# Norm statistics by accumulation, a reworked spatial gating and a richer scheduler model in a two-layer trunk kernel

## The chip, the cores and the metric

The kernel runs on the eight cores of one Trainium2 chip. The metric is the device time of one execution in microseconds (us), taken from the slowest core. Most executions agree within 0.3%. Some executions fall into a second, slower state, in which the cores of one die, sometimes of both, have a lower granted TensorE clock, that is, a lower share of the full clock at which the tensor engine may run (for example 0.93 to 0.95 against 0.98 to 0.99 in the run after that took 1251.35 us; in the run of `e12_best` that took 1307.13 us, 0.95 to 0.97 on one die and 0.89 to 0.90 on the other). A median that is given here is over all runs of its kernel, slow ones included, unless the text says otherwise.

Before the change the median was 1233.7 us (four runs, 1233.03 to 1415.23, the last one slow).

## The reference, cut to what matters

One inference step of two layers. Layer 0 mixes tokens with windowed attention beside a short gated convolution. Layer 1 mixes them with a chunked gMLP ("spatial gating"). Each is followed by a gated ConvFFN, and each sub-layer begins with an RMS norm with adaLN modulation.

```python
def rms_norm(x, g):
    y = x * lax.rsqrt(jnp.mean(x * x, axis=-1, keepdims=True) + EPS)
    return y * g

def modulate(x, g, shift, scale):
    return rms_norm(x, g) * (1 + scale) + shift

def gmlp_mixer(h, w_in, v_g, w_s, b_s, w_out):
    u, v = jnp.split(jax.nn.gelu(h @ w_in), 2, axis=-1)
    v = rms_norm(v, v_g).reshape(B, nc, CHUNK, GMLP_GROUPS, GMLP_GROUP_DIM)
    s = jnp.einsum('gts,bnsgc->bntgc', w_s, v) + b_s.T[:, :, None]
    return (u * s.reshape(B, T, GMLP_WIDTH)) @ w_out

def conv_ffn(h, w_up, conv_w, w_down):
    g, val = jnp.split(dwconv3(h @ w_up, conv_w), 2, axis=-1)
    return (jax.nn.silu(g) * val) @ w_down

# per layer: x = x + gate * mixer(modulate(x)); x = x + gate2 * conv_ffn(modulate(x))
```

The width is 1024, the FFN's inner width 2816. Each core holds 512 context tokens (tiles named P: `xP`, `hP`, `uP`) and some 1150 latent tokens with the halo that windows and convolutions need (tiles named S: `xS`, `hS`, `uS`).

## The kernel before

Activations lie feature-major: 1024 features are 8 chunks of 128 partitions, tokens run along the free axis. The sum over features of an RMS norm is therefore a sum over partitions. Before the change, it is done on the tensor engine: eight matmuls with a matrix of ones (value 1/1024) add the eight chunks of squares in PSUM, and the result is already broadcast over all partitions.

```python
class Norm:
    def sq(self, k, eng="act"):              # square of chunk k into the h tile
        P.act(h_(self.st, k), self.xf(k), AF.Square)
    def stat(self, k):                       # eight of these per norm
        if k == 0:
            self.b = BK.take(); BK.reserve(self.b)
        P.mm(bk(self.b, 0, self.st.n), ones, h_(self.st, k), start=(k == 0), stop=(k == KC - 1))
    def fin(self):                           # rsqrt as exp(-0.5 * ln(x))
        n = self.st.n
        r = self.rs[:, 0:n]
        P.act(r, bk(self.b, 0, n), AF.Ln, bias=eps)
        P.act(r, r, AF.Exp, scale=-0.5)
        BK.give(self.b)
    # apply(k): multiply by rs, then scale and shift, into h (the next matmul's operand)

def residual(nm, l, m, st, b, k, stat=True):   # after each output-projection block
    P.stt("dve", x_(st, k), bk(b, 0, st.n), mod_(l, m, k, st.j), x_(st, k), ALU.mult, ALU.add)
    if nm is not None:
        nm.sq(k)
        if stat:
            later(lambda: nm.stat(k), 2)
```

A norm's `fin` and its eight `apply` steps go into a queue, `side`, from which the main loop takes a few after every block of matmuls.

Spatial gating of layer 1, for 13 chunks of up to 128 tokens (v is token-major here, so its norm is along the free axis):

```python
def v_item(ch):                              # 16 matmuls, two Gelu, one sum of squares
    ...
    for i in range(2):
        P.act(ch["gv"][:, i * 512:(i + 1) * 512], bk(b2[i], 0, 512), AF.Gelu_apprx_tanh)
    P.add("dve", ... scalar_tensor_tensor(junk, gv, 1.0 / D, gv, mult, mult, accum_out=ssq[:, c:c+1]))
def v_stats(chs):                            # for a batch of 3 or 4 chunks
    P.act(rsv[:, a:z], ssq[:, a:z], AF.Ln, bias=eps)
    P.act(rsv[:, a:z], rsv[:, a:z], AF.Exp, scale=-0.5)
def v_norm(ch):
    P.stt("dve", ch["vn"].whole(), ch["gv"].whole(), rsv[:, c:c + 1], gvn.whole(), ALU.mult, ALU.mult)
def sp_item(ch):                             # 8 spatial matmuls, bias, gate product
    ...
        P.tt("dve", tv, <psum>, bsp..., ALU.add)
        P.tt("pool", uv, uv, tv, ALU.mult)
```

Finally, the program does not emit instructions in the order in which it is written. It records operations with their dependencies, and a list scheduler simulates the five engines with a cost model and takes, on each engine, the ready operation of the highest priority. The resulting order of each engine is fixed in the program. The model's numbers therefore matter only through the order which they produce:

```python
LAT = {"pe": 130.0, "act": 160.0, "dve": 130.0, "pool": 130.0, "sp": 100.0}   # ns, by producer
...
            else:
                busy = op.cost
                end = t + busy
...
                elif o.eng == op.eng and not o.is_dma:
                    r = end if e == "pe" or i not in o.raw else end + 90.0
                else:
                    r = end + LAT[e]
```

In the trace before, ScalarE loads an activation table at its first operation and wherever its work changes between `Ln`/`Exp` and the FFN's `Silu` or the gating's `Gelu`: 15 loads of 1.28 us. The model before knows nothing of that.

Of the kernel before, what the change touches and what calls it, by code (L numbers as in the profile page):

```python
# [9 lines left out]
F32 = mybir.dt.float32  # L10
BF16 = mybir.dt.bfloat16
AF = mybir.ActivationFunctionType
ALU = mybir.AluOpType
ESZ = {F32: 4, BF16: 2}
ENGINES = ("pe", "act", "dve", "pool", "sp")
LAT = {"pe": 130.0, "act": 160.0, "dve": 130.0, "pool": 130.0, "sp": 100.0}
DMA_RATE = 300.0


# [75 lines left out]
class Op:  # L95
    __slots__ = ("idx", "eng", "emit", "deps", "raw", "is_dma", "sig", "sem", "semval", "waits", "pre", "key",
                 "cost", "prio", "start", "pos", "end")

    def __init__(self, idx, eng, emit, is_dma):
        self.cost = 0.0  # L100
        self.prio = idx
        self.start = 0.0
        self.idx = idx
        self.eng = eng
        self.emit = emit
        self.deps = set()
        self.raw = set()
        self.is_dma = is_dma
        self.sig = False
        self.sem = None  # L110
        self.semval = None
        self.waits = ()
        self.pre = None
        self.key = None


class Prog:
# [112 lines left out]
    def schedule(self):  # L230
# [11 lines left out]
        free = {e: 0.0 for e in ENGINES}  # L242
        dma_free = 0.0
        for op in ops:
            if left[op.idx] == 0:
                heapq.heappush(wait[op.eng], (0.0, op.prio, op.idx))
# [3 lines left out]
        while ev:  # L250
# [16 lines left out]
            if op.is_dma:  # L267
                busy = 600.0 if e == "pool" else 60.0
                dma_free = max(dma_free, t + busy + 1300.0) + op.cost / DMA_RATE
                end = dma_free + 600.0  # L270
            else:
                busy = op.cost
                end = t + busy
            op.end = end
            free[e] = t + busy
            heapq.heappush(ev, (free[e], e))
            for j in succ[i]:
                o = ops[j]
                if op.is_dma:
                    r = end  # L280
                elif o.eng == op.eng and not o.is_dma:
                    r = end if e == "pe" or i not in o.raw else end + 90.0
                else:
                    r = end + LAT[e]
                ready[j] = max(ready[j], r)
# [13 lines left out]
    def act(self, out, in_, func, bias=None, scale=None, accum_out=None):  # L299
# [9 lines left out]
        if accum_out is not None:  # L309
            writes.append(accum_out)  # L310
            kw["accum_out"] = accum_out.ap
        return self.add("act", lambda e: e.activation(out.ap, in_.ap, func, **kw), reads=reads, writes=writes)  # L312

# [169 lines left out]
def build():  # L483
# [40 lines left out]
    with es:  # L524
# [214 lines left out]
        class Norm:  # L739
            def __init__(self, l, which, st, tmps, rs, x=None):  # L740
                self.l, self.w, self.st = l, which, st
                self.tmps, self.rs = tmps, rs
                self.xf = x if x is not None else (lambda k: x_(st, k))
                self.b = None

            def sq(self, k, eng="act"):
# [6 lines left out]
            def stat(self, k):  # L753
# [3 lines left out]
                P.mm(bk(self.b, 0, self.st.n), ones, h_(self.st, k), start=(k == 0), stop=(k == KC - 1))  # L757

            def fin(self):
                n = self.st.n  # L760
                r = self.rs[:, 0:n]
                P.act(r, bk(self.b, 0, n), AF.Ln, bias=eps)
                P.act(r, r, AF.Exp, scale=-0.5)
                BK.give(self.b)
# [25 lines left out]

        def residual(nm, l, m, st, b, k, stat=True):
            P.stt("dve", x_(st, k), bk(b, 0, st.n), mod_(l, m, k, st.j), x_(st, k), ALU.mult, ALU.add)
            if nm is not None:
                nm.sq(k)
                if stat:
                    later(lambda: nm.stat(k), 2)
# [285 lines left out]

        def oproj_item(l, key, src, st, nm, k, last, m=2, stat=True):
            w = use((key, k))
            b = BK.take()
            for kk in range(KC):
                P.mm(bk(b, 0, st.n), w[:, kk, :], src(st, kk), start=(kk == 0), stop=(kk == KC - 1))
            residual(nm, l, m, st, b, k, stat)
            if last:
                release((key, k))  # L1090
# [40 lines left out]
        def act_pair(out, b, ap, func, scale):  # L1131
            r = both(b, ap)
            return P.add("act", lambda e: e.activation(out.ap, ap, func, scale=scale), reads=r, writes=[out])  # L1133

# [50 lines left out]
        while al:  # L1185
            m, q = al.popleft()
            fill.append(lambda m=m, q=q: ada_item(0, m, q))
        nA = [Norm(0, 1, SP, None, None), Norm(0, 1, S0, None, None)]

        def oproj_a(st, nm, k):  # L1190
            assert all(bl.get("done") for bl in blocks[:8])
            oproj_item(0, "we", mx_, st, nm, k, False, stat=False)

# [40 lines left out]
        for i, nm in enumerate(nA):  # L1234
            nm.tmps, nm.rs = tA, rA[i]
            for k in range(KC):
                nm.stat(k)
            queue_apply(nm)
        ATAIL = O_W + NFC * 1664 * 2 - 12288
        tB = [P.tile(f"tB{i}", [128, NP], F32, ATAIL + 2048 * i) for i in range(4)]  # L1240
        rB = [P.tile(f"rB{i}", [128, NP], F32, ATAIL + 8192 + 2048 * i) for i in range(2)]
        nB = [Norm(0, 1, S1, tB, rB[0]), Norm(0, 1, S2, tB, rB[1])]
        for k in range(KC):
# [85 lines left out]
        F0 = ([SP, St(0, 0, 384)], [St(0, 384, 768), St(0, 768, 1152)])  # L1329
        flush()  # L1330
        for nm in nB:
            queue_apply(nm, PO8, AC8)

        def norms_l1(g, ft):
            if g == 0:
                tms = [ft[0][0], ft[0][1], ft[1][0], ft[1][1]]
                rss = [ft[2][0], ft[2][1]]
            else:
                tms, rss = l1t["tm"], l1t["rs"]
            return [Norm(1, 0, st, tms, rss[i]) for i, st in enumerate(F0[g])]  # L1340

# [36 lines left out]
        P.dma("sp", bsp.whole(), dr(d_bsp.ap()))  # L1378
        P.dma("pool", wst.whole(), dr(d_wst.ap()))
        for nm in keepB:  # L1380
            queue_apply(nm)

# [3 lines left out]
        def u_item(k, st, last):  # L1386
            w = use(("u", k))
            b = BK.take()
            for kk in range(KC):
                P.mm(bk(b, 0, st.n), w[:, kk, :], h_(st, kk), start=(kk == 0), stop=(kk == KC - 1))  # L1390
            P.act(u_(st, k), bk(b, 0, st.n), AF.Gelu_apprx_tanh)
            if last:
# [6 lines left out]
        def v_item(ch):  # L1399
            st, cbk = ch["st"], ch["c"]  # L1400
            ch["gv"] = gv[gi[0] % 6]
            ch["i"] = gi[0]
            gi[0] += 1
# [6 lines left out]
            for i in range(2):  # L1410
                P.act(ch["gv"][:, i * 512:(i + 1) * 512], bk(b2[i], 0, 512), AF.Gelu_apprx_tanh)
            c = ch["i"]
            P.add("dve", lambda e, a=ch["gv"], c=c: e.scalar_tensor_tensor(  # L1413
                junk.h[:, :], a.h[:, :], 1.0 / D, a.h[:, :], ALU.mult, ALU.mult, accum_out=ssq.h[:, c:c + 1]),
                reads=[ch["gv"].whole()], writes=[junk.whole(), ssq[:, c:c + 1]])

        def v_stats(chs):
            a, z = chs[0]["i"], chs[-1]["i"] + 1
            P.act(rsv[:, a:z], ssq[:, a:z], AF.Ln, bias=eps)
            P.act(rsv[:, a:z], rsv[:, a:z], AF.Exp, scale=-0.5)  # L1420

# [8 lines left out]
        def sp_item(ch):  # L1430
# [3 lines left out]
            for gh in range(2):  # L1434
# [9 lines left out]
                uv = ut[:, gh * 4:gh * 4 + 4, t0:t0 + nt_]  # L1444
                P.tt("pool", uv, uv, tv, ALU.mult)

        junk = P.tile("junk", [128, D], BF16, n1 + 10240)
        assert n1 + 10240 + 2048 <= O_END, n1 + 12288 - O_END

# [3 lines left out]
        side_all()  # L1453
        chP = [dict(st=SP, c=i) for i in range(4)]
        chS = [dict(st=G0, c=i) for i in range(9)]
        spq = deque()

        def v_batch(chs):
            for ch in chs:
                emit(lambda: v_item(ch))  # L1460
                if spq:
                    c2 = spq.popleft()
                    v_norm(c2)
                    emit(lambda: sp_item(c2))
            later(lambda: v_stats(chs))
            spq.extend(chs)

        v_batch(chP)
        v_batch(chS[0:3])
        for k in range(KC):  # L1470
            for st in (G1, G2):
                emit(lambda: u_item(k, st, st is G2))
            if spq and k % 2 == 1:
                c2 = spq.popleft()
                v_norm(c2)
                emit(lambda: sp_item(c2))
        v_batch(chS[3:6])
        v_batch(chS[6:9])
        release(("v", 0))
        release(("v", 1))  # L1480
        flush()
        H0, H1, H2 = St(0, 0, 383), St(0, 383, 704), St(0, 704, 1024)
        nA = [Norm(1, 1, st, l1t["tiles"][0:3], l1t["tiles"][3 + i]) for i, st in enumerate((SP, G0))]
        for k in range(KC):
            for st, nm in ((SP, nA[0]), (G0, nA[1])):
                emit(lambda: oproj_item(1, "wo", u_, st, nm, k, False))
                if spq and k < 4:
                    c2 = spq.popleft()
                    v_norm(c2)
                    emit(lambda: sp_item(c2))  # L1490
        flush()
        for nm in nA:
            queue_apply(nm)
        nB = [Norm(1, 1, st, None, None) for st in (G1, G2)]
        for k in range(KC):
# [167 lines left out]
```

## Time and profile before

| what | before |
|---|---|
| time, median of fast runs | 1233 us |
| tensor engine (PE) busy | 1142.7 us of 1232.2 (93%), 7225 matmuls |
| VectorE (DVE), ScalarE (ACT), GpSimd (POOL) busy | 763.3, 607.5, 423.9 us |
| norm statistics | 17 norms with 8 ones-matmuls each, 136 matmuls |

From the page of the profiled run (slowest core): the span, the busy time of each engine with its share and number of instructions, and by engine the chain of work that ended last.

```profile
span 1232.2 us, 21546 instructions; the slowest of 8 cores (1225.8 to 1232.2 us)
PE 1142.7 (93%) x7225; PEld 630.5 (51%) x7225; DVE 763.3 (62%) x1281; ACT 607.5 (49%) x1072; POOL 423.9 (34%) x489
...
PE 79%; DVE 8%; issue 5%; DMA 4%; ACT 4%; POOL 1%; DVEq 0%; ACTq 0%; POOLq 0%; SPq 0%
```

The kernel is bound by PE, and 79% of the last chain is matmul. There are two ways to gain: fewer matmuls, or less of the 89.5 us in which PE stands idle. The busy table by stretches of time tells where these are. Its first columns are the stretch and its length, then the busy time of each engine with the number of instructions, then the granted clock.

```profile
core 3: us, PE busy (x) PEld busy (x) DVE busy (x) ACT busy (x) POOL busy (x), PEclk, DMA share, GB/s
0.00:75.00 75.00, 26.80 (x226) 13.59 (x226) 26.62 (x58) 24.75 (x42) 17.08 (x30) 0.94 0.92 181
75.00:313.00 238.00, 214.32 (x1305) 99.03 (x1305) 148.79 (x251) 153.76 (x242) 72.66 (x84) 0.94 0.38 68
...
757.00:845.00 88.00, 79.86 (x496) 43.30 (x495) 57.60 (x71) 36.30 (x64) 38.95 (x37) 1.00 0.31 52
```

In the first 75 us weights and inputs arrive (DMA share 0.92), and PE idles 48 us. In projections and attention it idles 24 us, in spatial gating 8.1 us (88.00 less 79.86), between 375 and 660 us, in the first FFN, nothing.

The waits of PE in spatial gating (730 to 850 us), by what it waited for: total, number, longest.

```profile
PE ps L296 <- DVE vn L336: 5.2, 5, 1.7
PE ps L296 <- ACT uP L312: 1.8, 1, 1.8
PE ps L296 <- DVE tg L315: 1.6, 3, 0.7
...
```

So the wait that costs most is that for the normalised v (`vn`). Two things precede `vn`. One is the rsqrt on ScalarE with a table load before and behind it, as ScalarE's timeline shows (start, duration, instruction):

```profile
772.40 0.60 ACT L312 ACTIVATE gv<-ps 128x512 f32<-128x512 f32 x1 [1.13 <-PE ps L296]
773.00 1.28 ACT L312 ACT_TABLE_LOAD   x1
774.30 0.30 ACT L312 ACTIVATE rsv<-ssq,cf 128x4 f32<-128x4 f32 x1
774.68 0.20 ACT L312 ACTIVATE rsv<-rsv 128x4 f32<-128x4 f32 x1
774.91 1.28 ACT L312 ACT_TABLE_LOAD   x1
```

At the first of these loads one activation ends at 773.00 us and the next starts at 774.30, so this switch cost 1.30 us.

The other is the product on VectorE itself. The groups of instructions by shape (count, then busy us, then mean ns of one, then idle time before them):

```profile
L336 DVE SCALAR_TENSOR_TENSOR vn<-gv,rsv,gvn 128x1024 bf16<-128x1024 f32 x13 | 21.2, 1652 | 6.4 <-ACT rsv L312 6.4
L1413 DVE SCALAR_TENSOR_TENSOR junk<-gv 128x1024 bf16<-128x1024 f32 x13 | 18.8, 1443 | 29.0 <-ACT gv L312 29.0
L315 POOL TENSOR_TENSOR uS<-uS,tg 128x512 bf16<-128x512 bf16 x16 | 20.6, 1315 | 19.5 <-DVE tg L315 19.4
L312 ACT ACT_TABLE_LOAD x15 | 19.2, 1283 | 16.2 <-PE ps L296 6.3 <-DVE junk L1413 5.7 <-DMA cf<-cf 4.1
```

The mean of `vn` is 1652 ns, but single ones range from 1.27 us to 2.15 us, the long ones where a gate product of GpSimd (`uS<-uS,tg`) runs beside them.

### The profile page before, as it was taken

To read this page: it belongs to the slowest core of one execution; us is meant where nothing else is said; L and a number is where in the kernel's file an instruction comes from. 1 tells how busy PE (TensorE), PEld (TensorE's weight loads), DVE (VectorE), ACT (ScalarE), POOL (GpSimd) and SP (SyncE) were. 2 spreads that over 40 slices of the span, in tenths; PEclk is the share of its full clock that TensorE was granted. 3 is DMA by queue.
4 is the path that set the end of the run, shared out by engine and by line. 5 is a ranking of instruction groups with operands and counts; after the bars stand their busy time and mean duration, and the time that the engine had idled before them with its cause. 6 is when DMAs were issued, how large, how long until landed. Compare 5 with 4: busy or idle time off the path is not lost.

```text
span 1232.2 us, 21546 instructions; the slowest of 8 cores (1225.8 to 1232.2 us)
## 1 busy us (share of the span) xinstructions
PE 1142.7 (93%) x7225; PEld 630.5 (51%) x7225; DVE 763.3 (62%) x1281; ACT 607.5 (49%) x1072; POOL 423.9 (34%) x489
## 2 busy tenths in 40 slices
PE   1478899898999999999999999998999999999999
PEld 1235533333545555555555554544556555555566
DVE  3179765444679888888511522756788898893111
ACT  2257566667696555555312435443875555551000
POOL 2136512210374444444200321543554444442000
PEclk9889999989899999999999999999999999999999
DMA  9882254640313577776354560143306332225661
GB/s 182 173 199 44 35 86 67 103 71 1 52 18 57 96 123 138 124 134 119 65 103 86 92 131 7 21 68 59 52 1 103 55 65 50 48 48 110 141 136 56
DMA packets 32604, 102.27 MB, mean 83 GB/s; under 512 B 3312, under 2 KB 10096, under 8 KB 32112
## 3 DMA queue, kind: packets, MB, share of 16 engines
q0 software_dynamic: 23616, 85.21, 40.9%
q1 hardware_dynamic: 8880, 15.69, 3.9%
q8 instruction: 60, 0.98, 0.3%
q14 instruction: 48, 0.39, 0.1%
HBM read 179.27 MB, written 6.82 MB: 151 GB/s over the span
## 4 chain that ended last, share of the span: by engine, by line
PE 79%; DVE 8%; issue 5%; DMA 4%; ACT 4%; POOL 1%; DVEq 0%; ACTq 0%; POOLq 0%; SPq 0%
PE ps L296 79%; DMA w_ada<-ada 3%; DMA xS<-xs 1%; DVE cvt L336 1%; DVE nd L315 1%; DVE vn L336 1%; ACT pt L1133 1%; ACT L312 1%; ACT hS L312 1%; DVE pt L315 1%; DVE xS L336 0%; DVE nn L342 0%; DVE junk L1413 0%; DVE c L342 0%; DVE tm L315 0%
## 5 line engine op out<-in xcount | busy, mean ns | idle before, releaser
L336 DVE SCALAR_TENSOR_TENSOR ft<-ps,cf,ft 128x510 f32<-128x510 f32 (+5 forms) x704 | 424.3, 631 | 70.1 <-ACT ft L312 29.2
L296 PE MATMUL ps<-hS,w_up 128*128 128x386 bf16 (+4 forms) x2112 | 334.6, 318 | 0.1
L296 PEld LDWEIGHTS ps<-hS,w_up 128*128 128x128 bf16 x2112 | 206.2, 98 | 126.9 <-issue 0.6
L312 ACT ACTIVATE ft<-ps,cf 128x384 f32<-128x384 f32 (+4 forms) x354 | 200.3, 586 | 76.6 <-PE ps L296 76.0
L296 PE MATMUL ps<-hP,w_up 128*128 128x512 bf16 x704 | 159.7, 379 | 1.1 <-DVE ft L336 1.1
L312 ACT ACTIVATE ft<-ft 128x384 f32<-128x384 f32 (+4 forms) x178 | 95.6, 537 | 114.7 <-DVE ft L336 110.9
L336 DVE SCALAR_TENSOR_TENSOR xS<-ps,modv,xS 128x384 f32<-128x384 f32 (+3 forms) x96 | 56.6, 593 | 152.8 <-PE ps L296 152.7
L315 POOL TENSOR_TENSOR actT_a<-ft,ft 128x512 bf16<-128x512 f32 (+2 forms) x96 | 99.2, 1033 | 127.2 <-DVE ft L336 78.9
L296 PE MATMUL ps<-actT_a,w_dn 128*128 128x384 bf16 (+4 forms) x768 | 140.7, 333 | 0.8 <-DVE xS L336 0.8
L315 POOL TENSOR_TENSOR actT_b<-ft,ft 128x512 bf16<-128x512 f32 (+2 forms) x80 | 82.7, 1033 | 125.1 <-DVE ft L336 87.3
L296 PE MATMUL ps<-actT_b,w_dn 128*128 128x384 bf16 (+4 forms) x640 | 118.9, 333 | 0.0
L296 PEld LDWEIGHTS ps<-hP,w_up 128*128 128x128 bf16 x704 | 67.5, 98 | 76.4 <-issue 1.4
L296 PEld LDWEIGHTS ps<-actT_a,w_dn 128*128 128x128 bf16 x768 | 75.1, 98 | 56.1 <-issue 1.6
L296 PEld LDWEIGHTS ps<-actT_b,w_dn 128*128 128x128 bf16 x640 | 62.7, 98 | 45.7
L1133 ACT ACTIVATE pt<-ps 128x1024 bf16<-128x1024 f32 (+2 forms) x73 | 71.8, 983 | 28.2 <-PE ps L296 27.6
L312 ACT ACTIVATE hS<-xS 128x384 bf16<-128x384 f32 (+2 forms) x84 | 41.9, 509 | 79.1 <-DVE xS L336 77.1
L336 DVE SCALAR_TENSOR_TENSOR xP<-ps,modv,xP 128x512 f32<-128x512 f32 x32 | 24.0, 749 | 79.4 <-PE ps L296 79.3
L348 POOL DMA_DIRECT2D w_dn<-w_dn x32 | 17.8, 556 | 127.5 <-PE ps L296 127.5
L296 PE MATMUL ps<-hS,w_cv 128*128 128x386 bf16 (+2 forms) x288 | 57.9, 335 | 1.9 <-DVE modv L315 1.3
L296 PE MATMUL ps<-pt,vtok 128*128 128x512 bf16 (+2 forms) x154 | 44.6, 375 | 7.7 <-DVE pt L315 6.0
L312 ACT ACTIVATE hP<-xP 128x512 bf16<-128x512 f32 x28 | 17.3, 627 | 59.7 <-DVE xP L336 51.9
L348 POOL DMA_DIRECT2D w_ada<-ada x48 | 27.0, 565 | 48.1 <-PE ps L296 23.3
(164 smaller groups left out, 1297.3 us busy)
## 6 DMA issues: line engine op xcount, KB each, us to landing
w_ada<-ada POOLq DMA_DIRECT2D x48, 512.0 KB, 8.1
w_up<-w_up POOLq DMA_DIRECT2D x44, 512.0 KB, 7.1
w_dn<-w_dn POOLq DMA_DIRECT2D x32, 704.0 KB, 7.4
xS<-xs SPq DMA_DIRECT2D x2, 1536.0 KB, 10.0
w_cv<-w_cv POOLq DMA_DIRECT2D x4, 768.0 KB, 9.7
xP<-xp SPq DMA_DIRECT2D x1, 2048.0 KB, 11.4
w_we<-w_oe POOLq DMA_DIRECT2D x8, 256.0 KB, 4.6
w_u<-w_u POOLq DMA_DIRECT2D x8, 256.0 KB, 5.2
```

The source lines that it names most:

```text
L296: return self.add("pe", lambda e: e.matmul(out.ap, lhsT.ap, rhs.ap, start=start, stop=stop), reads=[lhsT, rhs], writes=[out])
L312: return self.add("act", lambda e: e.activation(out.ap, in_.ap, func, **kw), reads=reads, writes=writes)
L315: return self.add(eng, lambda e: e.tensor_tensor(out.ap, in0.ap, in1.ap, op), reads=[in0, in1], writes=[out])
L336: return self.add(eng, lambda e: e.scalar_tensor_tensor(out.ap, in0.ap, sc, in1.ap, op0, op1), reads=reads, writes=[out])
L348: op = self.add(q, lambda e: e.dma_start(out.ap, in_.ap), reads=[in_], writes=[out], is_dma=True)
L1133: return P.add("act", lambda e: e.activation(out.ap, ap, func, scale=scale), reads=r, writes=[out])
```

## The change

It has three parts, which touch different code.

**Accumulation.** In ten of the 17 norms GpSimd adds the squares of the chunks as they come (six adds), VectorE makes the last add, and one ones-matmul takes the place of eight. In layer 0 the second ("late") pair of FFN norms (tokens S1, S2) has its finish delayed by 12 empty steps of the side queue, to give its chain time.

**Gating.** The sum of squares moves from VectorE to ScalarE, the rsqrt from ScalarE's `Ln`/`Exp` to a Newton iteration on VectorE (nine small operations per pair of chunks), the gate product from GpSimd to VectorE. The chunks are processed in pairs, interleaved more finely with u blocks and output blocks. The first `Gelu` waits until both late norms before it have done their `Exp`.

**Scheduler.** The latency becomes a matrix of producer and consumer, mostly longer, and the same-engine latency rises from 90 to 190 or 200 ns. A change of activation table adds 2600 ns to an operation in the simulation.

```diff
-LAT = {"pe": 130.0, "act": 160.0, "dve": 130.0, "pool": 130.0, "sp": 100.0}
+LAT = {"pe": {"act": 160.0, "dve": 270.0, "pool": 270.0, "sp": 200.0},
+       "act": {"pe": 160.0, "act": 190.0, "dve": 220.0, "pool": 220.0, "sp": 200.0},
+       "dve": {"pe": 236.0, "act": 190.0, "dve": 190.0, "pool": 200.0, "sp": 200.0},
+       "pool": {"pe": 236.0, "act": 200.0, "dve": 200.0, "pool": 200.0, "sp": 200.0}}
+TABLES = {AF.Ln: "ln_exp", AF.Exp: "ln_exp", AF.Silu: "silu", AF.Gelu_apprx_tanh: "gelu"}
+TABLE_NS = 2600.0
@@ schedule @@
                 busy = op.cost
+                if op.table is not None and op.table != table:
+                    table = op.table
+                    busy += TABLE_NS
@@ Norm @@
+            def accum(self, k):
+                st, a = self.st, self.acc[:, 0:self.st.n]
+                if k == 1:
+                    P.tt("pool", a, h_(st, 0), h_(st, 1), ALU.add)
+                elif 1 < k < KC - 1:
+                    P.tt("pool", a, a, h_(st, k), ALU.add)
+                elif k == KC - 1:
+                    P.tt("dve", h_(st, 0), a, h_(st, k), ALU.add)
+            def stat1(self):
+                self.b = BK.take()
+                BK.reserve(self.b)
+                P.mm(bk(self.b, 0, self.st.n), ones, h_(self.st, 0))
             def fin(self):
+                if self.acc is not None:
+                    self.stat1()
@@ layer 0, before the FFN @@
         flush()
+        side.extend([lambda: None] * 12)
         for nm in nB:
             queue_apply(nm, PO8, AC8)
@@ spatial gating @@
-            P.add("dve", ... scalar_tensor_tensor(junk, gv, 1.0 / D, gv, mult, mult, accum_out=ssq...))
+            P.act(junk.whole(), ch["gv"].whole(), AF.Square, scale=1.0 / 32, accum_out=ssq[:, c:c + 1])
         def v_stats(chs):
-            P.act(rsv[:, a:z], ssq[:, a:z], AF.Ln, bias=eps)
-            P.act(rsv[:, a:z], rsv[:, a:z], AF.Exp, scale=-0.5)
+            x, h, t, y = (q[:, a:z] for q in small)
+            P.ts("dve", x, ssq[:, a:z], 1e-6, None, ALU.add)
+            P.ts("dve", <h as int32>, <x as int32>, 1, None, ALU.logical_shift_right)
+            P.ts("dve", <y as int32>, <h as int32>, -1, 0x5f3759df, ALU.mult, ALU.add)
+            for it in range(2):
+                P.stt("dve", t, y, -0.5, y, ALU.mult, ALU.mult)
+                P.tt("dve", t, t, x, ALU.mult)
+                P.stt("dve", rsv[:, a:z] if it == 1 else y, t, 1.5, y, ALU.add, ALU.mult)
@@ sp_item @@
-                P.tt("pool", uv, uv, tv, ALU.mult)
+                P.tt("dve", uv, uv, tv, ALU.mult)
... (cut: the order of v, u, spatial and output items, tile placement, acc tiles, table names on operations)
```

## The prediction

The length of a table load and what the v-norm takes beside GpSimd's products were measured before the change (1283 ns in the mean, 1.9 to 2.15 us against 1.27 us).

> **What bounds the kernel now.** The tensor engine: the engine table gives PE 1142.7 of 1232.2 us busy (93%), and the chain that ended last is 79% matmul. By the windows, PE's 89.5 us of idle lie so: 48 us in the first 75 us (weights and inputs arriving, not touched), 24 us in 75 to 313 (projections, attention), 2.5 us in 313 to 375, nothing in the first FFN, 12 us between 660 and 885 (8.1 of it in spatial gating, 757 to 845), then 2 to 4 us. The granted clock is below 1.00 only before 340 us.
>
> **What the change does.**
>
> 1. *Fewer statistics matmuls.* In ten RMS norms (three of 512 columns, seven of about 384) eight ones-matmuls become one; GpSimd adds the squares (six adds), VectorE makes the last add. In the PE timeline such a matmul takes 0.216 us (512) or 0.163 us (384) from start to start: 7 x (3 x 0.216 + 7 x 0.163) = 12.5 us of PE. In the down projections PE is 100% busy, so it counts in full; around 309 to 340 us it partly uncovers other waits. I count 10.5 us.
> 2. *No table switching in spatial gating.* The v statistics go from ScalarE Ln/Exp to a Newton iteration on VectorE, and Gelu waits for both norms' Exp. The timeline shows pairs of 1.28 us table loads at 739, 773, 789, 818 and one at 831 us, with PE waits of 0.3 to 1.8 us after them. [...]
> 3. *Moved work.* The sum of squares (13 x 1.44 us) goes from VectorE to ScalarE, the gate product (26, about 1.3 us each) from GpSimd to VectorE. The v-norm takes 1.27 us alone, 1.9 to 2.15 us beside GpSimd products. [...] Finer interleaving of v, spatial and output items gives PE filler. Items 2 and 3: of 12 us of idle, 7 come back.
> 4. *Scheduler model.* Longer, per-pair latencies and a table cost reorder the static instruction streams. The waits in 75 to 355 us (mask product 6.0, exp 5.9, QK-norm operand 4.1 us) are many short ones; I expect 5 of 24 us back, uncertain.
> 5. *New costs.* GpSimd gets 60 adds (0.9 to 1.5 us, some 70 us) for 33 us removed. The second pair of layer 0's FFN norms must finish its chain and starts 12 side slots later in the FFN's first 36 us, with 16 GpSimd multiplies (0.93 us) and table switches. I count 1 us of PE wait.
>
> **Sum.** 10.5 + 7 + 5 - 1 = 21.5 us: predicted 1212 us, range 1202 to 1222. Faster by over 2% (below 1209) 0.39, within 2% 0.60, slower 0.01.
>
> **What would show it.** Ones-matmuls of norms fall from 136 to 66 and PE busy by about 12 us; table loads from 15 to 7 to 10; PE idle in the spatial stage from 8 to 2 or 3 us; v-norm near 1.3 us; GpSimd busy near 460 us. If item 4 is wrong, PE idle before 313 us stays 72 us.
>
> **What would make it wrong.** GpSimd's chain may end late and stall the FFN's second group (near 370 us); Newton's nine dependent small VectorE operations per pair may make VectorE the limit of spatial gating; the new order may help attention far more (10 us) or hurt it.

## The result

| | before | after |
|---|---|---|
| median us (runs) | 1232.8 (16, 1231.03 to 1415.23) | 1209.1 (11, 1207.06 to 1396.67) |
| ratio | | 0.980, 95% interval 0.9786 to 0.9814 |

A ratio here is the mean time of one kernel's fast runs over the mean of the other's fast runs of the same rounds, so it is not quite the ratio of the medians quoted. Four of the eleven runs after were slow; the median of the seven fast ones is 1208.7 us. The gain is 2.0%, just on the line between "within 2%" and "faster by over 2%"; the interval contains the line.

The page after, the same parts:

```profile
span 1208.6 us, 21673 instructions; the slowest of 8 cores (1199.4 to 1208.6 us)
PE 1125.1 (93%) x7155; PEld 622.9 (52%) x7155; DVE 766.5 (63%) x1354; ACT 624.3 (52%) x1086; POOL 448.1 (37%) x523
...
PE 81%; DVE 6%; DMA 6%; issue 4%; ACT 3%; POOL 0%; DVEq 0%; ACTq 0%; POOLq 0%; SPq 0%
```

There are exactly 70 matmuls fewer, as counted. The DMA share of the chain rose from 4% to 6%, which becomes important below. In the windows, the stages have shifted by up to 27 us against the ones before. The row that lies inside spatial gating in both kernels may still be compared:

```profile
757.00:845.00 88.00, 85.78 (x552) 48.98 (x551) 67.30 (x141) 42.30 (x79) 19.96 (x25) 1.00 0.32 54
```

PE's idle time in it fell from 8.1 to 2.2 us. The waits of PE in spatial gating (735 to 862 us) after:

```profile
PE ps L307 <- ACT hS L323: 2.5, 4, 0.9
PE ps L307 <- DVE vn L349: 2.2, 2, 1.5
```

And the groups that answer to those shown before, by shape:

```profile
L349 DVE SCALAR_TENSOR_TENSOR vn<-gv,rsv,gvn 128x1024 bf16<-128x1024 f32 x13 | 17.1, 1356 | 0.5 <-DVE rsv L349 0.2
L328 DVE TENSOR_TENSOR uS<-uS,tg 128x512 bf16<-128x512 bf16 x16 | 12.6, 811 | 0.0
L323 ACT ACT_TABLE_LOAD x11 | 14.1, 1283 | 12.9 <-PE ps L307 6.8 <-DMA cf<-cf 4.0 <-DVE ft L349 2.0
```

The v-norm is down from 1652 to 1356 ns, table loads from 15 to 11, and the gate product takes 811 ns on VectorE instead of 1315 on GpSimd.

To say where the time went, fixed windows are of little use. I cut each core's span at the first matmul of each stage (read from the matmuls of each weight tile) and took the median of the eight cores. "Attention" includes its output projection, "gating" the output projection of layer 1; the last stage ends with the last matmul. The columns for the experiments are told below.

| stage, us | before | after | scheduler only | accumulation only | gating only | after, old scheduler |
|---|---|---|---|---|---|---|
| start-up | 156.9 | 153.3 | 154.9 | 157.7 | 157.4 | 157.7 |
| attention | 177.6 | 169.4 | 172.3 | 172.6 | 177.6 | 172.6 |
| FFN 0, up | 261.8 | 263.1 | 260.3 | 272.4 | 261.9 | 272.3 |
| FFN 0, down | 130.4 | 124.3 | 129.3 | 124.1 | 130.3 | 124.3 |
| u blocks | 26.4 | 25.2 | 24.5 | 25.6 | 24.6 | 24.7 |
| gating | 127.1 | 117.7 | 129.4 | 126.0 | 122.7 | 121.5 |
| FFN 1, up | 230.5 | 230.4 | 230.4 | 230.5 | 230.5 | 230.5 |
| FFN 1, down | 114.6 | 114.5 | 114.6 | 114.6 | 114.5 | 114.5 |

The medians of the stages fall by some 27 us, the time by 24, because the slowest core, not the median core, sets the time: after the change the cores' spans scatter from 1199.4 to 1208.6 us.

The first row needs a caution. In the kernel after and in six of the experiments on it (`e6` to `e11`), ScalarE, VectorE and GpSimd execute the same instructions in the same order up to 305 us. Yet their start-up medians lie between 152.9 and 158.1 us (the last one from the quiet die of a slow profile). The four kernels with the old scheduler model lie between 156.9 and 157.7 us. So a part of the 3.6 us by which start-up fell is chance; "The start-up of three cores" shows where it comes from. The attention row of those kernels scatters less: 169.4 to 170.5 us, without `e8_nb0mm`, which changes that stage.

### The profile page after: what moved, and what is told of

Read it like the earlier page. It is cut to its first block, busy times and chain, and to the rows that moved or that the text cites. A ratio compares the mean times of both kernels' runs of the same rounds, so it can differ in the third digit from the quotient of the medians.

```text
span 1208.6 us, 21673 instructions; the slowest of 8 cores (1199.4 to 1208.6 us)
## 1 busy us (share of the span) xinstructions
PE 1125.1 (93%) x7155; PEld 622.9 (52%) x7155; DVE 766.5 (63%) x1354; ACT 624.3 (52%) x1086; POOL 448.1 (37%) x523
## 4 chain that ended last, share of the span: by engine, by line
PE 81%; DVE 6%; DMA 6%; issue 4%; ACT 3%; POOL 0%; DVEq 0%; ACTq 0%; POOLq 0%; SPq 0%
PE ps L307 81%; DMA w_ada<-ada 3%; DMA xS<-xs 2%; ACT pt L1167 1%; DVE nd L328 1%; DVE nn L355 1%; ACT hS L323 1%; DVE tm L328 1%; DVE cvt L349 1%; DVE pt L328 0%; DMA w_q<-w_q 0%; DVE xS L349 0%; DVE cvt L328 0%; DVE tN L328 0%; DVE hS L328 0%
## 5 line engine op out<-in xcount | busy, mean ns | idle before, releaser
L349 DVE SCALAR_TENSOR_TENSOR ft<-ps,cf,ft 128x510 f32<-128x510 f32 (+5 forms) x704 | 416.2, 629 | 75.3 <-ACT ft L323 45.6
L323 ACT ACTIVATE ft<-ps,cf 128x384 f32<-128x384 f32 (+4 forms) x354 | 207.4, 592 | 130.2 <-PE ps L307 119.8
L307 PEld LDWEIGHTS ps<-hS,w_up 128*128 128x128 bf16 x2112 | 206.0, 98 | 129.3 <-issue 3.6
## 6 DMA issues: line engine op xcount, KB each, us to landing
w_cv<-w_cv POOLq DMA_DIRECT2D x4, 768.0 KB, 10.5
xP<-xp SPq DMA_DIRECT2D x1, 2048.0 KB, 11.2
```

Of the source, the lines that this page charges most:

```text
L307: return self.add("pe", lambda e: e.matmul(out.ap, lhsT.ap, rhs.ap, start=start, stop=stop), reads=[lhsT, rhs], writes=[out])
L323: op = self.add("act", lambda e: e.activation(out.ap, in_.ap, func, **kw), reads=reads, writes=writes)
L349: return self.add(eng, lambda e: e.scalar_tensor_tensor(out.ap, in0.ap, sc, in1.ap, op0, op1), reads=reads, writes=[out])
```

## The experiments

Twelve kernels were run, all with the right result, in three calls, each on another chip. The runs of before in them had medians of 1233.16, 1234.23 and 1233.33 us. The question was not whether the sum of the prediction was right (it was), but whether its terms were. The theory is a sum of independent terms: matmuls removed, gating's waits removed, scheduler better in attention. The rival is that the parts depend on each other.

### One part at a time

`e1_sched` is the kernel before with the scheduler part alone:

```diff
-LAT = {"pe": 130.0, "act": 160.0, ...}
+LAT = {"pe": {"act": 160.0, "dve": 270.0, ...}, ...}   # and the table cost of 2600 ns, same-engine 190 ns
```

> The kernel before with the scheduler part alone: the pair-wise latencies, the same-engine latency and the table cost; every operation stays. Theory A (the parts are nearly independent and add up, each of about the size that the stage times of the two traces suggest): start-up to the first attention exp about 153 us on the median core instead of 157, attention and output projection to the first FFN about 3 us shorter than 177.6, the other stages unchanged within 1 us; about 1227 us in all. Rival B (the new order pays only with the new operations, because it is the filler of the finer interleaving that it arranges): within 2 us of the kernel before, 1231 to 1235. [...]

Measured: 1225.7 us, ratio 0.9935 (0.992 to 0.9951). Start-up and attention gain 2.0 and 5.3 us, FFN 0 up 1.5 us, but gating *loses* 2.3 us.

`e2_accum` is the kernel before with the accumulation part alone:

```diff
-nA = [Norm(0, 1, SP, None, None), Norm(0, 1, S0, None, None)]
+nA = [Norm(0, 1, SP, None, None, acc=accs[0]), Norm(0, 1, S0, None, None, acc=accs[1])]
+# likewise for the other eight norms, with accum(), stat1() and the 12 empty side steps
```

> The kernel before with the GpSimd accumulation of the squares alone (ten norms, 70 matmuls fewer, the 12 empty side slots), old scheduler and old spatial gating. Theory A: matmul count down by 70, PE busy down by 12 us; down projection of layer 0 124.3 us instead of 130.4, attention stage about 4 us shorter, first FFN up projection 1 to 2 us longer, gating to second FFN about 2.5 us shorter; about 1222 us. Rival B (with the old latencies the GpSimd chains are ordered badly and what PE saves turns into waits): the down projection still gains 6 us, but attention and FFN stages give back over half; 1227 to 1231 us.

Measured: 1230.48 us, ratio 0.9977 (0.9959 to 0.9995). Less than 3 us come of 12.5 us of matmuls. Attention gains 5.0 us and FFN 0 down 6.3 us, the full price of the matmuls removed there and a little more, but FFN 0 up grows by 10.6 us and takes it back.

`e3_gate` is the kernel before with the gating part alone (its norms keep the eight matmuls):

```diff
-P.act(rsv...Ln); P.act(rsv...Exp); P.tt("pool", uv, uv, tv, ALU.mult)
+# Newton on VectorE, squares on ScalarE, product on VectorE, pairs, interleaving
```

> The kernel before with the spatial-gating part alone (Newton statistics on VectorE, squares on ScalarE, product on VectorE, pairs interleaved with output items, Gelu after both Exp), statistics by matmul and old scheduler. Theory A: the stage from the first v item to the second FFN takes about 120 us instead of 127, the u stage about 1 us less, start-up, attention and both FFNs unchanged; about 1225 us; table loads about 8 fewer. Rival B: with the old scheduler the stage keeps over half of its 8 us of PE idle, 1229 us or more.

Measured: lowest 1224.49 us, ratio 0.9938 (0.9916 to 0.9959); three of six runs were slow, so its median of 1269.23 says nothing. Gating gains 4.4 us and the u blocks 1.8.

`e4_oldsched` is the changed kernel with the old scheduler model:

```diff
-                    r = end + LAT[e][o.eng]
+                    r = end + LAT[e]                    # old LAT, 90 ns, no table cost
```

> The changed kernel with the old scheduler model (single latency per engine, no table cost). Theory A: start-up back at 157 us on the median core, attention 3 us longer than in the changed kernel, the down projection, the u stage and gating as in the changed kernel within 1 us; about 1215 us. Rival B: gating and the first FFN lose 2 us or more each without the new model, 1219 us or more.

Measured: 1225.48 us, ratio 0.9939 (0.9921 to 0.9956).

What follows: alone, the three parts gain 0.65, 0.23 and 0.62%, together 1.5%, or 18.5 us of 1233. The whole change gains 2.0%, or 24.7 us. The gap of 0.5% is more than the four intervals together allow (about 0.35%). The sum of independent terms has fallen. Above all, the scheduler part gains 8 us alone (0.65% of 1233) but some 17 us on top of the other two (0.9939 less 0.9800, of 1233). By the table its extra gain lies in FFN 0 up (272.3 to 263.1) and in gating (121.5 to 117.7, where alone it lost).

### What happens in the first FFN

The 10.6 us of `e2_accum` lie in the beginning of FFN 0. There the late pair of norms finishes (`Ln` and `Exp`, into tiles `rB`) while the FFN already runs its `Silu` on the same engine. The table loads on ScalarE between 338 and 372 us with accumulation and the old scheduler, core 2, and what lies around some of them:

```profile
339.32 1.28 ACT L312 ACT_TABLE_LOAD   x1 [2.03 <-DVE ft L336]
...
350.60 1.28 ACT L312 ACT_TABLE_LOAD   x1
351.90 0.58 ACT L312 ACTIVATE rB<-ps,cf 128x384 f32<-128x384 f32 x1
352.50 1.28 ACT L312 ACT_TABLE_LOAD   x1
353.79 0.63 ACT L312 ACTIVATE ft<-ft 128x512 f32<-128x512 f32 x1
354.43 1.28 ACT L312 ACT_TABLE_LOAD   x1
355.72 0.52 ACT L312 ACTIVATE rB<-rB 128x384 f32<-128x384 f32 x1
...
```

The scheduler has put a `Silu` (`ft<-ft`) between the `Ln` and the `Exp` of one norm, so that each of three neighbouring short operations (0.5 to 0.6 us) pays a load of 1.28 us. Three more loads follow (at 358.23, 365.80 and 371.04 us), six in all behind the first. PE's waits in 338 to 400 us of this kernel:

```profile
PE ps L296 <- ACT hS L312: 4.3, 5, 1.7
PE ps L296 <- DVE ft L336: 3.5, 3, 1.7
```

7.8 us, where the kernel before has PE wait 1.1 us. That explains 6.7 of the 10.6 us. More than half of the rest is the granted clock. Here are two rows of the busy table of the same core, at the end of these waits and behind them:

```profile
380.00:386.80 6.80, 4.78 (x15) 2.01 (x16) 4.86 (x9) 4.71 (x10) 3.98 (x5) 0.50 0.01 2
386.80:400.00 13.20, 13.20 (x82) 7.92 (x81) 11.65 (x21) 8.12 (x16) 7.19 (x9) 1.00 0.47 80
```

For 6.8 us the granted clock is 0.50. The 15 matmuls there take 0.32 us each, and those behind them 0.16 us, so about 2.4 us are lost. Every core of this run and of `e4_oldsched` has 6.8 us at half clock in this stage; before, after, `e1_sched` and `e10_fins` have none on any core. The loss comes with the long waits; that they cause it is not shown.

ScalarE produces `hS`, the FFN's next operand, and it makes the first pass over the PSUM results to which VectorE's taps then add (`ft`), so a late ScalarE reaches PE on both ways. `e4_oldsched` has the same pattern of seven loads (338.23 to 369.94 us on core 2) and the same 7.8 us of waits. With the new scheduler, the kernel after has four behind the first:

```profile
336.14 1.28 ACT L323 ACT_TABLE_LOAD   x1 [2.02 <-DVE ft L349]
346.24 1.28 ACT L323 ACT_TABLE_LOAD   x1
349.49 1.28 ACT L323 ACT_TABLE_LOAD   x1
359.43 1.28 ACT L323 ACT_TABLE_LOAD   x1
362.89 1.28 ACT L323 ACT_TABLE_LOAD   x1
```

Each of the two norms now has its `Ln` and `Exp` together, and PE waits 1.9 us there. But the new scheduler differs from the old one in latencies and in the table cost. `e9_notable` is the changed kernel with the new latencies and without the table cost:

```diff
-TABLES = {AF.Ln: "ln_exp", AF.Exp: "ln_exp", AF.Silu: "silu", AF.Gelu_apprx_tanh: "gelu"}
+TABLES = {}
```

> The changed kernel with an empty table map, so that the scheduler again knows no cost for switching activation tables; the new latencies stay. Theory E (the table cost is what keeps Ln and Exp of the late norms together between the Silu of the first FFN, and so what makes the accumulation pay): first FFN up projection near 270 us instead of 263, six table loads between 340 and 375 us instead of four, other stages within 1.5 us; total 1215 to 1219 us. Rival F (the latencies do it): up projection stays below 264.5 us, total 1208 to 1211 us.

Measured: lowest 1220.28 us, ratio 0.9891 (0.9875 to 0.9907). Its profile was taken in the slow state of die 0, so I read only cores 4 to 7: FFN 0 up 271.9 us, seven table loads in the same pattern as with the old scheduler (336.6 to 367.0 us on core 5), PE waits 7.3 us, and the same 6.8 us at half clock. On these cores attention takes 169.8 to 170.9 us, FFN 0 down 124.3 and gating 118 to 119, near those of the kernel after. So it is the table cost that keeps FFN 0 at 263.1 us, and it is worth about 0.9% of the whole by the ratios. That is 11 us, of which this stage shows 8.8; the start-up of this run was also 4.8 us later on the quiet die, in the same order. What the scheduler part gains on the other two in attention (172.6 to 170 us) and in gating (121.5 to 118 or 119) is there without it, and so comes of the latencies.

The model does not choose by table. By its code the 2600 ns only lengthen an operation in the simulation, which changes what is ready when. So it still leaves the two norms apart. `e10_fins` puts both finishes ahead of all `apply` steps of the late pair:

```diff
-for nm in nB:
-    queue_apply(nm, PO8, AC8)
+for nm in nB:
+    side.append(nm.fin)
+for nm in nB:
+    for k in range(KC):
+        side.append(lambda nm=nm, k=k: nm.apply(k, "pool", "act"))
```

> The changed kernel, with both late norms of layer 0's FFN finished together (Ln and Exp of both, then the sixteen multiplies), after the same 12 empty side slots: two activation table loads of 1.28 us fewer among the Silu of the first FFN. Theory E: the first FFN up projection goes from 263.1 to 260.5 to 262 us, other stages unchanged; total 1206.5 to 1209. Rival J (what is left there is GpSimd being full with the multiplies and products, not the table loads): stage stays at 262.8 us or more, total as the changed kernel.

Measured: 1208.0 us, ratio 0.9788 (0.977 to 0.9807). Table loads of the stage:

```profile
334.59 1.28 ACT L323 ACT_TABLE_LOAD   x1 [2.04 <-DVE ft L349]
344.69 1.28 ACT L323 ACT_TABLE_LOAD   x1
348.81 1.28 ACT L323 ACT_TABLE_LOAD   x1
```

Two loads are gone, PE has no wait left in 338 to 400 us, and FFN 0 up takes 260.4 us, 2.7 less than after. In the time this shows only in part, as long as the slowest core is set by something else (its fast runs scatter from 1204.94 to 1209.75 us, with a median of 1206.0). Its interval overlaps that of the kernel after, so the gain is shown in the stage and not in the time.

`e8_nb0mm` asks the opposite: is accumulation worth it for the late pair at all? It gives that pair its eight matmuls back and takes away the empty steps.

```diff
-nB = [Norm(0, 1, S1, tB, rB[0], acc=accs[2]), Norm(0, 1, S2, tB, rB[1], acc=accs[3])]
+nB = [Norm(0, 1, S1, tB, rB[0]), Norm(0, 1, S2, tB, rB[1])]
-        side.extend([lambda: None] * 12)
```

> The changed kernel with the statistics of the second norm pair of layer 0's FFN by eight matmuls again, and without the 12 empty side slots: the pair whose chain ends late. Theory A: attention and output projection 2 us longer (14 matmuls of 0.163 us), first FFN up projection 2 to 3 us shorter (260.5 us, no table switches inside it), total within 1.5 us of the changed kernel, 1207 to 1210. Rival: the chain costs nothing that matters, and the matmuls come back on top: 1210 to 1212.

Measured: 1214.04 us, ratio 0.9837 (0.9823 to 0.9851). FFN 0 up falls to 260.4 us, as with `e10_fins`, but attention with its output projection takes 175.2 us, 5.8 more than after. The 14 matmuls are worth 14 x 0.163 = 2.3 us at full clock; PE's waits between 295 and 345 us on core 3 have 0.9 us for the residual and 0.4 us for squares that the kernel after hasn't; and the granted clock in that stretch is only 0.88 to 0.89 in both (in the kernel after it is 0.56 from 298 to 305 us and 1.00 from there to 326). Of the remaining 2 us, about 1.6 are granted clock after all: over the whole stage, PE's matmuls lose 8.1 us to it on the median core, against 6.5 us in the kernel after (an estimate: the busy time under each reduced clock, times what it lacks to 1). The total of 1214 us lies outside both ranges. So here my "partly uncovers other waits" was the wrong way round: accumulation takes away waits too, and the late pair alone is worth 3 us net by the stages (5.8 less 2.7) and 4.6 us by the ratios. (The start-up of this run was 4.1 us later than that of the kernel after in the same order, so the larger figure may hold some chance.)

### What made spatial gating faster

The prediction put 7 us on two causes together, table switching and moved work. There is a 2 x 2 of sorts to take them apart, always with the new interleaving and the new scheduler. `e6_lnexp` gives the rsqrt back to ScalarE:

```diff
-# nine small VectorE operations
+P.act(rsv[:, a:z], ssq[:, a:z], AF.Ln, bias=eps)
+P.act(rsv[:, a:z], rsv[:, a:z], AF.Exp, scale=-0.5)
```

> The changed kernel with the v statistics by Ln and Exp on ScalarE again (the rest of the gating part stays: pairs, interleaving, squares on ScalarE, product on VectorE). Theory G (the table loads were the cause of the gating stalls): seven pairs of table loads of 1.28 us come back, and PE idle in the stage rises by 4 to 8 us; total 1213 to 1217. Rival H (the finer interleaving and the lag of one to two items hide the loads, and most of the gain came from it): stage within 2 us of the changed kernel's 117.7, total 1208 to 1211.

Measured: 1213.46 us, ratio 0.9825 (0.9811 to 0.9838), gating 119.6 us against 117.7. The table loads of the whole run rise from 11 to 27, and yet the stage loses only 1.9 us, net of what the Newton chain itself had cost. (In the kernel after, on core 7 from 750.95 us on, the nine operations of a pair are busy 0.16 to 0.17 us each and start some 0.27 us apart, so some 40% of the chain is no work.) The stage is thus as rival H has it, the total as theory G has it; the start-up of this run was 2.6 us later, which is within the scatter of kernels with the same order.

`e7_poolprod` gives the gate product back to GpSimd:

```diff
-                P.tt("dve", uv, uv, tv, ALU.mult)
+                P.tt("pool", uv, uv, tv, ALU.mult)
```

> The changed kernel with the gate product alone back on GpSimd. If the block between VectorE and GpSimd matters in the end, the v-norm median rises from 1.28 to 1.8 us or more and the gating stage from 117.7 to 119.5 us or more, total 1211 to 1214. If VectorE has slack there, the stage stays within 1 us and the total at 1208 to 1211.

Measured: 1221.14 us, ratio 0.9903 (0.9885 to 0.9921), gating 128.6 us: this one line is worth 10.9 us of the stage. But not as I thought, and the total lies outside both ranges. I expected the v-norm to be slowed to 1.8 us by a block between the two engines, as before the change it took 1.9 to 2.15 us beside GpSimd's products and 1.27 us alone; its median stayed at 1.28 us. GpSimd's and VectorE's timelines on core 0 show the victim:

```profile
752.18 2.29 POOL L328 TENSOR_TENSOR uP<-uP,tg 128x512 bf16<-128x512 bf16 x2 [24.95 <-DVE tg L328]
759.72 4.53 POOL L328 TENSOR_TENSOR uP<-uP,tg 128x512 bf16<-128x512 bf16 x4 [5.25 <-DVE tg L328]
```

```profile
753.47 1.02 DVE L339 TENSOR_SCALAR small<-small 128x2 int32<-128x2 int32 x1
754.60 0.17 DVE L340 TENSOR_SCALAR small<-small 128x2 int32<-128x2 int32 x1
...
762.13 1.01 DVE L339 TENSOR_SCALAR small<-small 128x2 int32<-128x2 int32 x1
763.25 1.02 DVE L340 TENSOR_SCALAR small<-small 128x2 int32<-128x2 int32 x1
764.38 0.16 DVE L349 SCALAR_TENSOR_TENSOR small<-small 128x2 f32<-128x2 f32 x1
```

A Newton step on two columns takes 0.16 us where GpSimd is idle. The first one here starts at 753.47 and ends at 754.49; GpSimd's pair of products ends at 752.18 + 2.29 = 754.47. The tiny operation has waited for the large one to end. Two in a row wait for two of the next four products in the same way. The operations behind the products are quick again. One of them at 821.56 us even took 2.15 us. The chain comes late, `vn` comes late, and PE waits for `vn` 10.9 us on this core (2.2 us on the slowest core after). Operations with one input and with two meet this wait: of the eleven Newton operations over 0.9 us on this core, four are `TENSOR_SCALAR`, with one input, and seven have two. In proportion it hit the smallest ones hardest: they went from 0.16 to 1.0 us, and `vn` went from 1.27 to 2.15. The granted clock plays a part here as well: it is 0.5 for 3.4 to 10.2 us of this stage, depending on the core, and never below 1.00 in the kernel after.

`e11_mixonly` undoes all three moves (Ln/Exp, squares on VectorE, product on GpSimd) and keeps the new interleaving:

```diff
-P.act(junk.whole(), ch["gv"].whole(), AF.Square, scale=1.0 / 32, accum_out=ssq[:, c:c + 1])
+P.add("dve", ... scalar_tensor_tensor(junk, gv, 1.0 / D, gv, mult, mult, accum_out=ssq...))
-# Newton
+P.act(rsv...Ln); P.act(rsv...Exp)
-                P.tt("dve", uv, uv, tv, ALU.mult)
+                P.tt("pool", uv, uv, tv, ALU.mult)
```

> The changed kernel with all moved operations of spatial gating back where they were (statistics by Ln and Exp on ScalarE, sum of squares on VectorE, product on GpSimd), so that only the interleaving in pairs, the output items as filler and the wait of Gelu are left of the gating part. Theory G (moving the work and the table loads made most of the gain): stage from the first v item to the second FFN back to 124 us or more (the kernel before: 127.1, of which 2.7 us are statistics matmuls), total 1215 or more. Rival H (the interleaving made it): stage 119 to 121 us, total 1210 to 1213. The v-norm beside GpSimd products takes 1.8 us or more in the median again instead of 1.28.

Measured: 1215.79 us, ratio 0.9862 (0.9846 to 0.9877), gating 124.6 us, as theory G has it. Beside a GpSimd operation the v-norm takes 1.82 us in the median (32 of 104 on the eight cores), elsewhere 1.28 us.

| gating, us | product on VectorE | product on GpSimd |
|---|---|---|
| Newton on VectorE | 117.7 (after) | 128.6 (`e7_poolprod`) |
| Ln/Exp on ScalarE | 119.6 (`e6_lnexp`) | 124.6 (`e11_mixonly`, squares on VectorE too) |

Before, the stage took 127.1 us; less its 14 statistics matmuls (7 x (0.216 + 0.163) = 2.65 us), that is 124.4. Against this the finer interleaving by itself bought nothing (124.6). But two more things differ between these two kernels. One is the scheduler: under the new model alone (`e1_sched`) the old gating takes 129.4 us, less the matmuls 126.8, and against that the interleaving bought 2.2 us. The other is the granted clock, which is 0.5 for 6.8 us of this stage on six of the eight cores of `e11_mixonly` and on no core before; the other two cores take 122.3 and 122.7 us. So the interleaving bought between nothing and about 2 us; the runs don't separate it further. The absence of table loads bought 1.9 us, and the move of the products, with that of the squares, 5.0 us (124.6 to 119.6), or 2.9 us against the two cores at full clock. Newton on VectorE gains only in company: with the product on GpSimd it makes things worse (128.6). The right column isn't a clean pair, because `e11_mixonly` has its squares on VectorE as well; how much the squares do alone is not tested.

### The start-up of three cores

After the change cores 1, 5 and 7 reach attention late (156.0, 157.9 and 158.6 us, against 151.7 to 154.4 of the others), and they are the slowest. ScalarE's timeline on core 7:

```profile
65.86 0.71 ACT L323 ACTIVATE hS<-tm,modv,gmod 128x385 bf16<-128x385 f32 x1 [1.03 <-DVE tm L328]
73.92 0.53 ACT L323 ACTIVATE hS<-xS 128x384 bf16<-128x384 f32 x1 [7.35 <-DMA xS<-xs]
```

It stands for 7.35 us in front of the second block of latent tokens. On core 3 the same instruction starts at 68.22 us. The load was issued at 57.8 us on core 7 and at 57.0 on core 3; it took 16.0 us to land on core 7 and 11.1 at most on core 3. What differs is the load of the first convolution weights (768 KB), which GpSimd issues at 62.00 us on core 7 and 63.38 on core 3. On cores 1, 5 and 7 it follows the token load within 5 us (3.0 to 4.8), and the token load needs 15.1 to 16.0 us; on the others it follows after 5.6 us or more and the token load needs at most 12.6. That is a correlation, and not the full rule: before the change core 7 had a distance of 4.6 us, and its token loads took 11.1 us at most.

The other kernels that issue these loads in this order (`e1_sched` and `e6` to `e11`) make 64 cores with those of the kernel after. On 26 of them the weights follow within 5 us, and on 25 of these the token load takes over 13 us (median 15.6). On 28 they follow after 5.5 us or more, and on 2 of these it takes over 13 us (median 10.7); the ten between are mixed. The medians of these two groups for the start of attention are 157.5 and 152.9 us. How many cores are late, and which, differs from run to run (three here, five in `e8_nb0mm`). This is the chance in the start-up row above.

`e5_cvwait` makes the weights wait for the tokens, as a test of theory C, that their load is what lengthens the token load:

```diff
 load("sp", xS[:, :, 385:769], d_xs[1].ap())
-load_w()
+issue(wq[0], after=seq[-1:])
+seq.append(wq.popleft()["op"])
```

> The changed kernel, with one edit: the load of the first convolution weights waits for the second token load to land, instead of for the third query weight load. In the changed kernel's trace three of eight cores (1, 5, 7) have the second token load landing 15 to 16 us after its issue instead of 10 to 11, their ScalarE and VectorE stand in front of the squares of those tokens until 74 us, and they reach the first attention exp at 156 to 159 us instead of 152; the slowest core sets the time. Theory C [...]: all cores reach the first exp at 151 to 154 us, the load lands in 9 to 11 us on all cores, total 1203 to 1206 us. Rival D (the lateness is chance between cores, or the weights are needed at once): the spread of 5 us or more stays, or all cores move to 156 us or later; 1208 us or more.

Measured: 1207.86 us, ratio 0.9783 (0.9769 to 0.9797). The second token load now takes 9.5 to 11.4 us on all cores, and all reach attention between 154.7 and 156.6 us. So it is shown that the weights' load lengthened the token load of the late cores (15.1 to 16.0 us in the kernel after); by what way is not. But neither range was met, and the gain is only about 2 us, with overlapping intervals of the two kernels, since the weights come later and are then waited for: the fast cores lost what the slow ones won.

### Both corrections

`e12_best` is the kernel after with `e5_cvwait` and `e10_fins`:

```diff
+issue(wq[0], after=seq[-1:]); seq.append(wq.popleft()["op"])     # weights after tokens
+side.append(nm.fin) for both late norms, then the applies        # no Silu between
```

> Both edits that pointed to a gain: the first convolution weights wait for the second token load (that run: 1207.9 us, all cores at the first exp at 155 us), and both late norms finished together. If they add up: 1204 to 1206.5 us, up projection 260.5 to 262 us, start-up spread below 3 us. If the start-up edit only moves the wait, 1207 to 1209.

Measured: 1202.6 us (1202.31 to 1307.13), ratio 0.9754 (0.9736 to 0.9771). It beats both kernels, is clearly over the 2% line, and gains more over the kernel after than either correction alone, probably as no late core hides the other correction any more: the spans of the eight cores now lie between 1198.1 and 1201.1 us. Its stages: 154.6, 169.0, 260.4, 124.3, 25.2, 117.3, 230.4, 114.5 us. The total is better than the range and the up projection as expected; but the start of attention still spreads by 4.1 us (151.7 to 155.8), where less than 3 was expected.

## Why the prediction was right, and where its terms were not

The time, 1209.1 us against 1212 predicted, lies well inside the range of 1202 to 1222. The terms, as the prediction numbers them:

1. *Fewer statistics matmuls, 10.5 us.* Right, and a little small. 70 matmuls are gone. In FFN 0 down the stage gained 6.1 us, of which 28 matmuls are 7 x (0.216 + 3 x 0.163) = 4.9 us. With accumulation alone attention gained 5.0 us, the full 4.9 us of its 28 matmuls. The deduction for "partly uncovers other waits" was not needed (`e8_nb0mm`). The caveat is the stage next door, under 5.
2. *No table switching.* As a count nearly right: 11 loads for the 7 to 10 predicted; four of the 11 belong to the late norms in FFN 0, of which two can be avoided (`e10_fins`). As a cause of time too large: the loads in gating cost 1.9 us (16 loads of 1.28 us, `e6_lnexp`). PE had other work for most of the time in which ScalarE loaded tables.
3. *Moved work.* Right in direction; it is the larger share of the two. PE's idle time in the window fell from 8.1 to 2.2 us, as foretold (2 or 3), the v-norm to 1356 ns mean. The whole of 2 and 3 is 9.4 us in gating less its 2.65 us of matmuls, and 1.2 us in the u blocks: 8 us for the 7 predicted. But 3.8 of these come of the scheduler (121.5 to 117.7, under 4); alone, `e3_gate` gained 4.4 and 1.8 us. "Finer interleaving" bought between nothing and 2 us by itself, and the mechanism in `e7_poolprod` was the blocked Newton chain, not a slow v-norm.
4. *Scheduler model, 5 of 24 us back.* This is the step that failed, and in its mechanism. It expected the "many short" waits in 75 to 355 us to come back, and they did not: up to the first FFN matmul PE idles 71.5 us before and 70.6 us after (medians of the eight cores). That stretch is shorter all the same, by 11.1 us in the median (334.5 to 323.4). The matmuls removed are 4.9 us of it. `e4_oldsched` has the same matmuls and takes 330.1 us; of the 6.7 us that the new model gains on it, waits make 1.7 and a higher granted clock some 5 (the time that PE's busy matmuls lose to it, estimated as above, is 16.3 us there and 11.2 us after). So a gain of about the size predicted came by another way, partly by the chance of the start-up; why the clock is higher with the new order is not shown. What it left out lies outside attention and appears only when the other two parts are there: 9.2 us in FFN 0 (272.3 to 263.1), which is the table cost (`e9_notable`), and 3.8 us in gating, most of it from the latencies.
5. *New costs, 1 us of PE wait.* The kernel after has 1.9 us of PE wait in that stretch, 0.8 more than before, and 1.3 us more in the stage: right, but only because of 4. Under the same order and without that chain (`e8_nb0mm`) the stage takes 260.4 us, so the chain itself costs 2.7 us; with the old scheduler the same code costs 10.6 us. The prediction named this risk under "what would make it wrong" (the chain ends late and stalls the FFN), but put it on GpSimd's chain; it was ScalarE's tables. GpSimd's 60 adds took 60 us rather than 70, and its busy time 448.1 us rather than 460.

So the sum was right with some luck: one term came true by another mechanism, and the others held because the parts were combined as the author of the change had combined them. A prediction of the accumulation part alone from the same terms would have been wrong by some 7 us (10.5 less 1, against 2.8 measured). By the test for 4 (if 4 is wrong, PE's idle time before 313 us stays at 72 us) it was wrong: core 7, the slowest after, has 73 us, and the median of the eight cores is 70.1 us before and 70.6 after. Core 3 alone would mislead: its idle time up to the first FFN matmul is 338 - 264.8 = 73.2 us before and 322 - 254.1 = 67.9 us after, but it is the slowest core of the one run and the fastest of the other.

What stays open: why a token load takes longer when the weights follow it within 5 us; why the granted clock falls to 0.5 in some stretches, and less with the new order; what ScalarE's squares and the finer interleaving gain by themselves. PE's busy time fell by 17.6 us where the matmuls removed explain 12.5; most of the rest is the granted clock before the first FFN (15.4 us lost before, 11.2 after, in the median).

## What to carry to other kernels

Where the order of instructions is fixed by a model at build time, a change's cost must be read with its order: the same accumulation made the stage next door 10.6 us longer under one order and 2.7 us under another (263.1 against 260.4 without the late chain). And a wait may cost more than itself: the 7.8 us of waits in `e2_accum` came with 6.8 us at half clock. When work is taken from the bottleneck and put on a chain across three other engines, look at where that chain ends and which other work of the same engine it lands in. And do not put chains of tiny dependent VectorE operations beside large GpSimd products: each tiny one can wait for a whole product (in `e7_poolprod` 0.16 us became 1.0 us and more, with 10.9 us of PE waits for `vn` on core 0).
